# A two-block network on one core: a fixed TensorE order in the mixers' second stage, and earlier first outputs in the recurrent phase

## The chip, the cores and the metric

One core of one Trainium2 chip runs the whole program. The metric is the device time of one execution in microseconds (us). The kernel before takes 2088.3 us, the median of 3 runs (2087.17 to 2094.09). TensorE multiplies matrices, VectorE (DVE) and ScalarE (ACT) do the elementwise work, GpSimd (POOL) a little of it, and SyncE issues the loads of the weights.

## The reference

256 rows of 1024 features pass through ten phases in turn: attention, a feed-forward phase, a recurrent block, a feed-forward phase, and then twice a feed-forward phase, a hybrid mixer and a feed-forward phase. The change touches the recurrent block and the two mixers.

```python
def recurrent_block(h, w_in, conv_w, conv_b, w_a, b_a, w_x, b_x, lam, w_out):
    xr, gate = jnp.split(h @ w_in, 2, axis=-1)
    xr = centred_depthwise_conv(xr, conv_w, conv_b)
    y = rg_lru(xr, ..., reverse=False) + rg_lru(xr, ..., reverse=True)
    return (y * jax.nn.gelu(gate)) @ w_out

def hybrid_mixer(x, ...):
    ...
    ya = sliding_window_attention(...) @ w_branch_a
    ...
    o = gated_delta_rule(qb, kb, vb, g, beta)
    o = rms_norm(o) * dn_norm_g * jax.nn.silu(z)
    yb = o @ w_branch_b
    gate_a, gate_b = jnp.split(jax.nn.sigmoid(gate_raw), 2, axis=-1)
    return (gate_a * ya + gate_b * yb) @ w_out
```

The delta rule needs, for every head and chunk, the inverse of a lower triangular matrix; `t_inv` is applied to the values and the keys.

## The kernel before

All weights come as tiles of 128 x 1024 numbers in the order of use (`items_of`); `get` fetches them two at a time and splits each into a rounded half `hi` (ACT, L365) and a rest `lo` (DVE, L369), up to four tiles ahead of the one in use, into six buffers of each. A product of a weight tile is then three matmuls for every 128 rows, two with `hi` and one with `lo` (`up_mm`, L393 to L395; `mv_mm`, L429 to L431).

**Who sets the order.** The program is traced in the order of the Python code, and a list scheduler then places each engine's instructions by readiness and priority under its own cost model. Within a region under `tc.manual_schedule(engines={PE})` TensorE instead keeps the order of the code. An engine executes its own instructions strictly in the order placed.

**The mixers' second stage** (`ph_mix`, L1603 to L1618). `diag` inverts the 16 x 16 diagonal blocks of 16 units at once in 14 steps, each a shuffle (L1322), a multiply (L1323) and a subtract (L1324) on DVE. `blocks(0)` spreads the result into `B` (L1598). `double(bt)` then joins the blocks to 32, 64 and 128 in six steps: it transposes `B` into `D` on DVE (L1340), and alternates small matmuls of 32 x 32 or 64 x 64 (L1351, L1357 and L1360, L1370, L1381 and L1382, L1390, L1395, output `dq`) with copies and subtractions on DVE and ACT. `chunks(bt)` is the delta rule itself (L1415 to L1434, output `f`). `bt` is one of two halves of the heads. Between two of these steps stands `filler(1)`, one tile of work that depends on none of them: a branch product (output `py`, 24 matmuls), a quarter of z (output `z`, 12 matmuls of 512 columns), or a gate (output `pu`, 24 matmuls). Under the scheduler's free choice a filler may also run before the step that it follows in the code.

**The recurrent phase** (`ph_rnn`, L921 to L1078). For each of four groups of three channel tiles, `group` computes the two recurrences' gates by matmuls (output `gp`) and a long chain on ACT and DVE, `scans` runs six scans (L1029) and adds the two directions into `ys` (L1031), `gate(t)` makes one gate tile (`gl`, L1035), and `outs(g)` multiplies the two and splits the product into `tT` (ACT L382, DVE L384), which `down` multiplies into the four accumulators `acc` (L429 to L431, 12 matmuls for each of three tiles). In the code the order at the end is: `scans` of group 2, `group(3)`, `scans` of group 3, `outs(0)` and `down(0)`, three gates, `outs(1)` and `down(1)`, three gates, the rest.

Of the kernel before, what the change touches and what calls it, by code (L numbers as in the profile page):

```python
# [287 lines left out]
def fused_kernel(ctx, tc, x, wst, adaw, ada0, rows, rowc, cols, vecs, relb, cst, m1, rope, oh, out, phases=PH_ALL):  # L288
# [148 lines left out]
    def up(ph, *it):  # L437

        if (ph,) + it in head:
            return head.pop((ph,) + it)  # L440
        w = get(ph, *it)
        ps = ps_up()
        hT = state["hT"]
        if ph[:3] in ("mlp", "ffn"):
            up_wide(w, lambda kk: hT[:, kk, :], ps)
            return ps
        ps = ps[:, 0:256]
        if (ph,) + it in RAW:
            up_raw(w, ps)
        else:  # L450
            up_mm(w, lambda kk: hT[:, kk, :], ps)
        return ps
# [475 lines left out]
    def ph_rnn(ph, nxt):  # L928
# [91 lines left out]
        def scans():  # L1020

            g, rs, ii, aa = todo.pop()
            for d in range(2):
                r, i, a = rs[d], ii[d], aa[d]
                for t in range(3):
                    o, da, du = r[:, t, :], a[:, t, :], i[:, t, :]
                    if d == 1:
                        o, da, du = o[:, ::-1], da[:, ::-1], du[:, ::-1]
                    V.tensor_tensor_scan(out=o, data0=da, data1=du, initial=0.0, op0=ALU.mult, op1=ALU.add)  # L1029
            ys[g] = po.tile([128, 3, 256], F32, tag="ys", bufs=2, name="ys")  # L1030
            V.tensor_tensor(out=ys[g], in0=rs[0], in1=rs[1], op=ALU.add)  # L1031

        def gate(t):
            gl[t] = po.tile([128, 256], F32, tag="gl", bufs=6, name="gl")
            S.activation(out=gl[t], in_=up(ph, "g", t), func=AF.Gelu_apprx_tanh)  # L1035

        def outs(g):
            for tt in range(3):
                t = 3 * g + tt
                o = gl.pop(t)  # L1040
                V.tensor_tensor(out=o, in0=o, in1=ys[g][:, tt, :], op=ALU.mult)
                tT[t] = po.tile([128, 512], F32R, tag="tT", bufs=5, name="tT")
                split(tT[t][:, 0:256], tT[t][:, 256:512], o)
# [8 lines left out]
        while n < len(seq):  # L1052
            k, t = seq[n]
            if k == "x":
                conv(t)
            elif k == "b":
                if t:
                    scans()
                group(t // 3)
                if t == 9:  # L1060
                    scans()
                n += 2
            elif k == "g":
                gate(t)
                if t >= 10 and xs_todo:
                    xs_todo.pop(0)()
            else:
                g = t // 3
                outs(g)
                if g == 1:  # L1070
                    es.close()
                    xs_todo = x_scale()
                if g == 2:
                    for f in xs_todo:
                        f()
                    while side:
                        side.pop(0)()
                    ln_open(ph, nxt)  # L1078
                down(g)
                n += 2  # L1080
            n += 1
# [25 lines left out]
    def ph_mix(ph, nxt):  # L1107
# [291 lines left out]
        def chunks(bt):  # L1399

            H0 = 4 * bt
            A, ai, tl = fr[bt]
            C, v = BC[bt][1], vk[bt]
            m4 = lambda: p3.tile([128, 4, 128], F32, tag="m4", bufs=5, name="m4")

            def four(f):
                pv = ps_acc("f4").rearrange("p (u m) -> p u m", u=4)
                for h in range(4):
                    f(pv[:, h, :], h)
                return pv  # L1410
            w1, wt, kt = m4(), m4(), m4()
            for h in range(4):
                for c in range(2):
                    S.activation(out=v[:, h, c, :], in_=v[:, h, c, :], func=AF.Copy, scale=cf[:, c, H0 + h, 3:4])
            S.activation(out=kt, in_=four(lambda o, h: T.transpose(o, kq[H0 + h][:, 0, 0:128], idn)), func=AF.Copy)  # L1415
            S.activation(out=w1, in_=four(lambda o, h: T.matmul(o, lhsT=C[:, h, :], rhs=v[:, h, 0, :], start=True, stop=True)), func=AF.Copy)
            V.tensor_tensor(out=wt, in0=w1, in1=tl.unsqueeze(2).to_broadcast([128, 4, 128]), op=ALU.mult)
            yield
            S1 = m4()
            S.activation(out=S1, in_=four(lambda o, h: T.matmul(o, lhsT=kt[:, h, :], rhs=wt[:, h, :], start=True, stop=True)), func=AF.Copy)  # L1420
            V.tensor_copy(out=v[:, :, 0, :], in_=four(lambda o, h: T.matmul(o, lhsT=ai[:, h, :], rhs=w1[:, h, :], start=True, stop=True)))
            yield
            R, qs = m4(), m4()
            pk = four(lambda o, h: T.matmul(o, lhsT=kq[H0 + h][:, 0, 128:256], rhs=S1[:, h, :], start=True, stop=True))
            for h in range(4):
                V.scalar_tensor_tensor(out=R[:, h, :], in0=pk[:, h, :], scalar=cf[:, 1, H0 + h, 2:3], in1=v[:, h, 1, :], op0=ALU.mult, op1=ALU.add)
            pq = four(lambda o, h: T.matmul(o, lhsT=kq[H0 + h][:, 1, 128:256], rhs=S1[:, h, :], start=True, stop=True))
            V.tensor_tensor(out=qs, in0=pq, in1=eg[:, 1, H0:H0 + 4].unsqueeze(2).to_broadcast([128, 4, 128]), op=ALU.mult)
            yield
            w2 = m4()  # L1430
            S.activation(out=w2, in_=four(lambda o, h: T.matmul(o, lhsT=C[:, 4 + h, :], rhs=R[:, h, :], start=True, stop=True)), func=AF.Copy)
            yield
            po = four(lambda o, h: T.matmul(o, lhsT=ai[:, 4 + h, :], rhs=w2[:, h, :], start=True, stop=True))
            V.tensor_tensor(out=v[:, :, 1, :], in0=qs, in1=po, op=ALU.add)  # L1434
            yield

        def norm_o(cc):

            hs = slice(4 * cc, 4 * cc + 4)
            b4 = lambda m: m.unsqueeze(2).to_broadcast([128, 4, 128])  # L1440
            for c in range(2):
                o = vk[cc][:, :, c, :]
                sq = p3.tile([128, 4, 128], F32, tag="m4", bufs=5, name="sqo")
                f = p2.tile([128, 2, 4], F32, tag="f", bufs=2, name="f")
                q = qn[:, c, hs]
                S.activation(out=sq, in_=o, func=AF.Square)
                V.tensor_reduce(out=f[:, 0], in_=sq, axis=AX.X, op=ALU.add)
                V.tensor_tensor(out=f[:, 1], in0=q, in1=q, op=ALU.mult)
                V.scalar_tensor_tensor(out=f[:, 0], in0=f[:, 0], scalar=1.0 / 128.0, in1=f[:, 1], op0=ALU.mult, op1=ALU.mult)
                V.tensor_scalar(out=f[:, 0], in0=f[:, 0], scalar1=1e-6, scalar2=None, op0=ALU.add)  # L1450
                G.tensor_tensor(out=f[:, 0], in0=f[:, 0], in1=mhalf[:, 0:4], op=ALU.pow)
                V.scalar_tensor_tensor(out=f[:, 0], in0=f[:, 0], scalar=0.5, in1=q, op0=ALU.mult, op1=ALU.mult)
                V.tensor_tensor(out=o, in0=o, in1=b4(f[:, 0]), op=ALU.mult)
                V.tensor_tensor(out=o, in0=o, in1=zst[cc, c], op=ALU.mult)
# [23 lines left out]
        for j in range(3):  # L1478
            hi, lo = get(ph, "va", j)
            for kk in range(3 * j, min(3 * j + 3, 8)):  # L1480
                s = slice((kk - 3 * j) * VW, (kk - 3 * j) * VW + VW)
# [104 lines left out]
        def filler(n):  # L1586
            for _ in range(n):
                f = next(fi, None)
                if f:
                    f()  # L1590
# [5 lines left out]
        def blocks(bt):  # L1596
            B = p3.tile([128, 8, 32], F32, tag="B", name="B")
            V.tensor_tensor(out=B.rearrange("p u (e j) -> p u e j", j=16),  # L1598
                            in0=cs[:, K_P16:K_P16 + 32].rearrange("p (e j) -> p e j", j=16).unsqueeze(1).to_broadcast([128, 8, 2, 16]),
                            in1=dg["b"][:, 8 * bt:8 * bt + 8, :].unsqueeze(2).to_broadcast([128, 8, 2, 16]), op=ALU.mult)  # L1600
            BC[bt] = B, p3.tile([128, 8, 128], F32, tag="C", bufs=2, name="C")

        blocks(0)  # L1603
        filler(1)
        for _ in double(0):
            filler(1)
        blocks(1)
        steps = [double(1), chunks(0)]
        while steps:
            for s in list(steps):  # L1610
                if next(s, "end") == "end":
                    steps.remove(s)
            filler(1)
        norm_o(0)
        for _ in chunks(1):
            filler(1)
        filler(99)
        norm_o(1)  # L1618
        es3.close()
        es2.close()  # L1620
# [158 lines left out]
```

## Time and profile before

| | before |
|---|---|
| median of 3 runs | 2088.3 us |
| the profiled execution's own time | 2087.69 us |
| its span, first to last instruction | 2086.0 us |
| TensorE busy | 97% of the span |
| weight loads on TensorE | 85% |
| DVE, ACT, POOL busy | 73%, 54%, 6% |
| mean granted TensorE clock | 0.990 of full |

The span is what the trace covers; some 1.7 us lie around it. Busy time of TensorE is modelled, since matmuls overlap: 97% says that TensorE is rarely without work, not that it works at its peak. A stretch at a granted clock of 0.5 counts as busy and does half as much in it.

### The profile page before, as it was taken

What the parts mean: (1) busy time and instruction counts of PE and PEld (TensorE: products, weight loads), DVE (VectorE), ACT (ScalarE), POOL (GpSimd) and SP (SyncE); (2) the same over time, 40 slices, a digit from 0 to 9 for tenths busy, and PEclk for the clock granted to TensorE, in tenths of its full rate; (3) what the DMA queues carried; (4) which work ended last, traced back from release to release, by engine and by line L of the source; (5) the groups of instructions that cost most, each with busy time, mean ns of one, the idle gap of its engine ahead of it and who ended that gap; (6) DMA issues with size and microseconds to landing.
All of it is one profiled execution on the core that took longest, in us unless ns stands there. A gap on an engine that the chain in (4) does not pass through costs nothing. (4 is left out here: it accounts for less than half of the span.)

```text
span 2086.0 us, 34685 instructions
## 1 busy us (share of the span) xinstructions
PE 2027.6 (97%) x13786; PEld 1777.3 (85%) x13786; DVE 1516.6 (73%) x2735; ACT 1116.8 (54%) x1995; POOL 122.3 (6%) x157
## 2 busy tenths in 40 slices
PE   6999999989999999999999999999999999999998
PEld 4788888978888888888989888888889888998886
DVE  2689989987667666789956766676668897667665
ACT  3554446874544555477644455545546774445553
POOL 0000000000000000021011000000001111100000
PEclk9999999999999999999989999999999998999999
DMA  8978884355673655454424465555546434355552
GB/s 335 336 265 329 319 319 183 129 198 187 217 254 131 241 190 194 172 182 140 157 81 180 161 224 195 187 195 189 188 156 215 136 141 157 123 201 182 194 190 81
DMA packets 67698, 409.67 MB, mean 196 GB/s; under 512 B 8240, under 2 KB 8544, under 8 KB 27088
## 3 DMA queue, kind: packets, MB, share of 16 engines
q1 hardware_dynamic: 59952, 383.25, 50.5%
q0 software_dynamic: 7440, 24.03, 3.6%
q8 instruction: 108, 1.77, 0.3%
q14 instruction: 54, 0.44, 0.1%
q10 hardware_dynamic: 144, 0.18, 0.0%
HBM read 406.34 MB, written 4.24 MB: 197 GB/s over the span
## 5 line engine op out<-in xcount | busy, mean ns | idle before, releaser
L369 DVE TENSOR_TENSOR lo<-raw,hi 128x1024 fp32r<-128x1024 f32 (+2 forms) x689 | 729.1, 1069 | 308.8 <-ACT hi L365 299.1
L365 ACT ACTIVATE hi<-raw 128x1024 fp32r<-128x1024 f32 x578 | 605.3, 1053 | 338.2 <-PE pu L402 73.9
L402 PE MATMUL pu<-hT,hi 128*128 128x512 f32 x1760 | 439.2, 392 | 0.0
L402 PEld LDWEIGHTS pu<-hT,hi 128*128 128x128 f32 x1760 | 324.6, 188 | 65.2 <-issue 0.4
L429 PE MATMUL acc<-hi,tT 128*128 128x512 f32 x688 | 271.6, 396 | 3.2 <-ACT tT L382 3.0
L430 PE MATMUL acc<-hi,tT 128*128 128x512 f32 x688 | 271.6, 395 | 0.0
L393 PE MATMUL pu<-hT,hi 128*128 128x256 f32 x928 | 271.4, 292 | 0.0
L431 PE MATMUL acc<-lo,tT 128*128 128x512 f32 x688 | 270.2, 393 | 0.0
L395 PE MATMUL pu<-hT,lo 128*128 128x256 f32 x928 | 265.5, 286 | 2.3 <-DVE lo L369 2.3
L394 PE MATMUL pu<-hT,hi 128*128 128x256 f32 x928 | 265.5, 286 | 0.0
L404 PEld LDWEIGHTS pu<-hT,lo 128*128 128x128 f32 x1760 | 240.2, 191 | 17.1
L404 PE MATMUL pu<-hT,lo 128*128 128x256 f32 x1760 | 245.6, 283 | 0.0
L393 PEld LDWEIGHTS pu<-hT,hi 128*128 128x128 f32 x928 | 178.9, 193 | 12.9 <-issue 10.6
L382 ACT ACTIVATE tT<-r 128x256 fp32r<-128x256 f32 x152 | 63.1, 416 | 235.6 <-DVE r L918 136.9
L394 PEld LDWEIGHTS pu<-hT,hi 128*128 128x128 f32 x928 | 179.1, 193 | 3.0 <-issue 2.6
L395 PEld LDWEIGHTS pu<-hT,lo 128*128 128x128 f32 x928 | 178.9, 193 | 2.7 <-DVE lo L369 2.5
L429 PEld LDWEIGHTS acc<-hi,tT 128*128 128x128 f32 x688 | 130.0, 189 | 29.6 <-ACT tT L382 5.0
L431 PEld LDWEIGHTS acc<-lo,tT 128*128 128x128 f32 x688 | 129.8, 189 | 27.7 <-issue 0.4
L430 PEld LDWEIGHTS acc<-hi,tT 128*128 128x128 f32 x688 | 130.1, 189 | 24.4 <-DVE tT L384 1.6
L688 PE MATMUL hd<-h,raw 128*128 128x128 f32 x960 | 111.4, 276 | 0.0
L688 PEld LDWEIGHTS hd<-h,raw 128*128 128x128 f32 x960 | 109.5, 192 | 1.1
L384 DVE TENSOR_TENSOR tT<-r,tT 128x256 fp32r<-128x256 f32 x152 | 64.6, 426 | 54.8 <-ACT tT L382 54.8
(398 smaller groups left out, 2755.2 us busy)
## 6 DMA issues: line engine op xcount, KB each, us to landing
raw<-wst SPq DMA_DIRECT2D x316, 1024.0 KB, 4.8
aw<-adaw SPq DMA_DIRECT2D x80, 512.0 KB, 6.5
aw<-ada SPq DMA_DIRECT2D x16, 512.0 KB, 7.6
bias<-bias_d POOLq DMA_DIRECT2D x32, 192.0 KB, 2.8
g<-rows POOLq DMA_DIRECT2D x10, 512.0 KB, 4.7
b<-rows POOLq DMA_DIRECT2D x10, 512.0 KB, 5.7
bias_d<-ext_d POOLq DMA_DIRECT2D x1, 2048.0 KB, 20.2
gbc<-g_d POOLq DMA_DIRECT2D x4, 512.0 KB, 4.4
```

The costliest lines, as they stand in the source:

```text
L365: S.activation(out=hi[:, 0:n], in_=r, func=AF.Copy)
L369: V.tensor_tensor(out=lo[:, c:c + m], in0=r[:, c:c + m], in1=hi[:, c:c + m].bitcast(F32), op=ALU.subtract)
L384: (eng or V).tensor_tensor(out=dlo, in0=src, in1=dhi.bitcast(F32), op=ALU.subtract)
L393: T.matmul(ps, lhsT=hi[:, c], rhs=r[:, 0:256], start=kk == 0, stop=False)
L394: T.matmul(ps, lhsT=hi[:, c], rhs=r[:, 256:512], start=False, stop=False)
L395: T.matmul(ps, lhsT=lo[:, c], rhs=r[:, 0:256], start=False, stop=kk == KT - 1)
L402: T.matmul(ps, lhsT=hi[:, kk * 128:kk * 128 + 128], rhs=rhs(kk), start=kk == 0, stop=False)
L404: T.matmul(ps[:, 0:256], lhsT=lo[:, kk * 128:kk * 128 + 128], rhs=rhs(kk)[:, 0:256], start=False, stop=kk == KT - 1)
L429: T.matmul(ps, lhsT=th, rhs=hi, start=first, stop=False)
L430: T.matmul(ps, lhsT=tl, rhs=hi, start=False, stop=False)
L431: T.matmul(ps, lhsT=th, rhs=lo, start=False, stop=last)
L688: T.matmul(ps[:, half * 128:half * 128 + 128], lhsT=w[:, kk * 128:kk * 128 + 128], rhs=state["h32", half][:, kk, :], start=kk == 0, stop=k ...
```

## The change

Two independent edits. In both mixers the second stage goes under `tc.manual_schedule` for TensorE, so that `filler(1)` stays between the steps where the code has it. In the recurrent phase `outs(0)` moves ahead of `group(3)`, and `scans` of group 3 moves from right behind `group(3)` to behind the gate of tile 8. No arithmetic is added or removed.

```diff
             elif k == "b":
                 if t:
                     scans()
+                if t == 9:
+                    outs(0)
                 group(t // 3)
-                if t == 9:
-                    scans()
                 n += 2
             elif k == "g":
                 gate(t)
+                if t == 8:
+                    scans()
                 if t >= 10 and xs_todo:
                     xs_todo.pop(0)()
             else:
                 g = t // 3
-                outs(g)
+                if g:
+                    outs(g)
...
-        blocks(0)
-        filler(1)
-        for _ in double(0):
+
+        with tc.manual_schedule(engines={mybir.EngineType.PE}):
+            blocks(0)
             filler(1)
-        blocks(1)
-        steps = [double(1), chunks(0)]
-        while steps:
-            for s in list(steps):
-                if next(s, "end") == "end":
-                    steps.remove(s)
-            filler(1)
-        norm_o(0)
-        for _ in chunks(1):
-            filler(1)
-        filler(99)
+            for _ in double(0):
+                filler(1)
+            blocks(1)
+            steps = [double(1), chunks(0)]
+            while steps:
+                for s in list(steps):
+                    if next(s, "end") == "end":
+                        steps.remove(s)
+                filler(1)
+            norm_o(0)
+            for _ in chunks(1):
+                filler(1)
+            filler(99)
         norm_o(1)
```

Lines from L1062 on stand three, and from L1606 on five, higher in the changed kernel.

**First place: TensorE at the start of a mixer's second stage.** Before, from the first branch tile to the second step of `double(0)`; the lines left out are the rest of 96 matmuls `py` (four tiles), 48 `z` (four) and 11 `pu`:

```order
L393 MATMUL py<-oT,hi 128x256
...
L429 MATMUL z<-hi,hT 128x512
...
L393 MATMUL pu<-hT,hi 128x256
...
L1351 MATMUL dq<-D,A 32x16 x32
L395 MATMUL pu<-hT,lo 128x256
...
L1357 MATMUL dq<-P,B 32x16 x32
L1360 MATMUL dq<-B,P 32x16 x32
L1370 MATMUL dq<-D,A 32x32 x16
```

In the changed kernel, from the same branch tile; the lines left out are the rest of 48, 24 and 24 matmuls `py` (two tiles, one, one) and of 12 `z`:

```order
L393 MATMUL py<-oT,hi 128x256
...
L1354 MATMUL dq<-D,A 32x16 x32
L393 MATMUL py<-oT,hi 128x256
...
L1360 MATMUL dq<-P,B 32x16 x32
L1363 MATMUL dq<-B,P 32x16 x32
L393 MATMUL py<-oT,hi 128x256
...
L1373 MATMUL dq<-D,A 32x32 x16
L429 MATMUL z<-hi,hT 128x512
```

Ahead of the first step of `double(0)` stand two tiles where eight and a half stood, and behind every later step a whole tile. The other mixer reads the same.

**Second place: DVE at the end of `diag` in a mixer.** Before, from the eighth subtract to the transpose; left out are the steps between, with three more `lo`:

```order
L1324 TENSOR_TENSOR dgb<-dgb,dgs 128x16x8
L369 TENSOR_TENSOR lo<-raw,hi 128x1024
L1322 STREAM_SHUFFLE dgs<-dgb 128x256
...
L1323 TENSOR_TENSOR dgs<-dgs,dga 128x16x14
L369 TENSOR_TENSOR lo<-raw,hi 128x1024
L1324 TENSOR_TENSOR dgb<-dgb,dgs 128x16x14
L1598 TENSOR_TENSOR B<-cs,dgb 128x256
L1576 SCALAR_TENSOR_TENSOR zs<-zs,z 128x512
L1340 STREAM_TRANSPOSE D<-B 128x256
```

In the changed kernel; left out are only shuffles, multiplies and subtracts:

```order
L1327 TENSOR_TENSOR dgb<-dgb,dgs 128x16x8
L1325 STREAM_SHUFFLE dgs<-dgb 128x256
L1326 TENSOR_TENSOR dgs<-dgs,dga 128x16x9
...
L1327 TENSOR_TENSOR dgb<-dgb,dgs 128x16x14
L1601 TENSOR_TENSOR B<-cs,dgb 128x256
L1343 STREAM_TRANSPOSE D<-B 128x256
L1355 TENSOR_SCALAR P<-dq,cs 128x8x16
```

The five `lo` that stood between the last steps of `diag` now stand behind the transpose; up to the eighth multiply both orders are the same.

**Third place: DVE in the recurrent phase, behind the chain of the last group.** Before:

```order
L1014 SCALAR_TENSOR_TENSOR r<-q,r 128x768
L384 TENSOR_TENSOR tT<-gl,tT 128x256
L369 TENSOR_TENSOR lo<-raw,hi 128x1024
L1017 TENSOR_TENSOR i<-i,r 128x768 x2
L1029 SCALAR_TENSOR_TENSOR r<-a,i 128x256 x6
L369 TENSOR_TENSOR lo<-raw,hi 128x1024
L1031 TENSOR_TENSOR ys<-r 128x768
L369 TENSOR_TENSOR lo<-raw,hi 128x1024 x4
L384 TENSOR_TENSOR tT<-gl,tT 128x256 x3
```

In the changed kernel:

```order
L1014 SCALAR_TENSOR_TENSOR r<-q,r 128x768
L369 TENSOR_TENSOR lo<-raw,hi 128x1024 x2
L1017 TENSOR_TENSOR i<-i,r 128x768 x2
L369 TENSOR_TENSOR lo<-raw,hi 128x1024 x2
L1029 SCALAR_TENSOR_TENSOR r<-a,i 128x256 x2
L369 TENSOR_TENSOR lo<-raw,hi 128x1024 x2
L1029 SCALAR_TENSOR_TENSOR r<-a,i 128x256 x4
L384 TENSOR_TENSOR tT<-gl,tT 128x256
L1031 TENSOR_TENSOR ys<-r 128x768
L384 TENSOR_TENSOR tT<-gl,tT 128x256 x2
```

The third `tT` of the first outputs, the first `L384` before, has moved ahead of the whole chain of the last group, on ACT too; the six scans now let the `lo` of the gates through, and still stand ahead of the first `tT` of the second outputs.

## Rows read from the trace of the kernel before

**Rows 1.** The page, busy time of each engine:

```profile
PE 2027.6 (97%) x13786; PEld 1777.3 (85%) x13786; DVE 1516.6 (73%) x2735; ACT 1116.8 (54%) x1995; POOL 122.3 (6%) x157
```

**Rows 2.** Stretches of both mixers: us, busy PE PEld DVE ACT POOL, PEclk, DMA, GB/s:

```profile
1030.10:1048.60 18.50, 18.21 (x109) 16.12 (x108) 17.94 (x45) 8.41 (x9) 1.17 (x3) 1.00 0.65 227
1048.60:1069.50 20.90, 19.14 (x408) 17.32 (x408) 5.63 (x11) 7.42 (x15) 4.82 (x6) 0.59 0.26 96
1069.50:1119.50 50.00, 50.00 (x574) 47.13 (x575) 30.36 (x58) 23.56 (x37) 4.98 (x6) 1.00 0.31 111
...
1750.70:1769.30 18.60, 17.95 (x408) 16.28 (x408) 5.53 (x11) 7.31 (x15) 4.86 (x6) 0.63 0.28 107
```

**Rows 3.** The same view: stretches at one granted clock, and a wait without a fall:

```profile
126.00:140.00 14.00, 11.01 (x81) 9.76 (x80) 13.18 (x29) 8.69 (x14) 1.57 (x2) 1.00 0.32 112
...
434.66:438.07 3.41, 3.41 (x9) 2.69 (x9) 1.99 (x3) 3.38 (x4) 0.00 (x0) 0.50 0.16 29
444.90:448.31 3.41, 3.41 (x17) 3.41 (x17) 3.41 (x4) 1.56 (x3) 1.28 (x2) 0.50 0.22 23
1052.47:1069.54 17.07, 16.19 (x203) 14.61 (x204) 3.18 (x6) 6.35 (x13) 0.95 (x3) 0.50 0.19 63
1755.62:1769.27 13.65, 13.65 (x172) 12.35 (x171) 2.92 (x6) 5.25 (x10) 0.51 (x2) 0.50 0.22 78
```

**Rows 4.** Timeline of TensorE in both mixers: start, us, instruction, idle before it:

```profile
1024.34 0.36 PE L393 MATMUL py<-oT,hi 128*128 128x256 f32 x1
...
1030.17 0.28 PE L393 MATMUL py<-oT,hi 128*128 128x256 f32 x1
...
1119.50 0.27 PE L1462 MATMUL pt<-cs,vk 128*128 128x128 f32 x1
...
1726.45 0.36 PE L393 MATMUL py<-oT,hi 128*128 128x256 f32 x1
...
1819.33 0.27 PE L1462 MATMUL pt<-cs,vk 128*128 128x128 f32 x1
```

**Rows 5.** Timeline of DVE in the first mixer, the last steps of `diag`:

```profile
1032.38 1.21 DVE L369 TENSOR_TENSOR lo<-raw,hi 128x1024 fp32r<-128x1024 f32 x1
...
1034.04 0.29 DVE L1324 TENSOR_TENSOR dgb<-dgb,dgs 128x128 f32<-128x128 f32 x1
...
1039.00 0.45 DVE L1322 STREAM_SHUFFLE dgs<-dgb 128x256 f32<-128x256 f32 x1
1039.48 0.34 DVE L1323 TENSOR_TENSOR dgs<-dgs,dga 128x176 f32<-128x176 f32 x1
...
1041.75 0.36 DVE L1323 TENSOR_TENSOR dgs<-dgs,dga 128x192 f32<-128x192 f32 x1
1042.14 0.36 DVE L1324 TENSOR_TENSOR dgb<-dgb,dgs 128x192 f32<-128x192 f32 x1
...
1048.11 0.44 DVE L1340 STREAM_TRANSPOSE D<-B 128x256 f32<-128x256 f32 x1
```

**Rows 6.** Timeline of TensorE at the end of the recurrent phase:

```profile
434.46 1.93 PE L429 MATMUL acc<-hi,tT 128*128 128x512 f32 x4 [2.86 <-ACT tT L382]
...
444.70 0.43 PE L395 MATMUL pu<-hT,lo 128*128 128x256 f32 x1 [2.28 <-DVE lo L369]
...
451.56 0.63 PE L429 MATMUL acc<-hi,tT 128*128 128x512 f32 x2
...
459.96 0.28 PE L393 MATMUL pu<-hT,hi 128*128 128x256 f32 x1
```

**Rows 7.** Timeline of ACT and DVE there:

```profile
434.32 1.05 ACT L365 ACTIVATE hi<-raw 128x1024 fp32r<-128x1024 f32 x1
...
436.68 1.48 ACT L1015 ACTIVATE r<-r 128x1536 f32<-128x1536 f32 x1
...
439.94 3.59 DVE L1029 TENSOR_TENSOR_SCAN r<-a,i 128x256 f32<-128x256 f32 x6
...
449.97 1.09 DVE L384 TENSOR_TENSOR tT<-gl,tT 128x256 fp32r<-128x256 f32 x3
```

## The prediction, made before the changed kernel ran

> **What bounds the kernel now.** I read the page first: TensorE is busy 97% of the span [rows 1], so time can only be won where it waits or where its clock is low. I then asked for the busy time by stretch, for those whose granted clock is not 1.00. Besides the start and the end of the program there are four [rows 3]: two of 3.41 us in the recurrent phase and one in each mixer, of 17.07 and 13.65 us, all at 0.50, the lower of the clock's two levels (1.2 of 2.4 GHz). The reader is to see in rows 2 that the long ones lie right where `double(0)` runs: after 1048.6 TensorE is handed small matmuls with little between them, while in the 18.5 us ahead of that it is busy for 18.21 us with large tiles, and DVE is busy for 17.94. From 1069.5 to 1119.5 it is busy without a gap at the full clock. So the free order spends eight and a half fillers while `diag` is still being computed, and has few left for `double(0)`.
>
> The timeline gives each stage's length, from the first branch tile to the turn of the output: 1119.50 - 1024.34 = 95.16 us and 1819.33 - 1726.45 = 92.88 us [rows 4]. In the recurrent phase the timeline shows two waits [rows 6]: 2.86 us for the ACT half of the third `tT`, 2.28 us for the `lo` of a gate tile.
>
> **The mixers, step by step.** First what the stage costs without loss. In the first mixer 16.19 us of work are done at half the clock [rows 3], which at the full one take 8.1; 20.90 - 19.14 = 1.76 us are idle behind 1048.6 and 18.50 - 18.21 = 0.29 ahead of it [rows 2]. The loss is 8.1 + 1.8 + 0.3 = 10.2 us, and the work 95.2 - 10.2 = 85.0. The second mixer: 13.65 / 2 = 6.8, plus 18.60 - 17.95 = 0.65 and some 0.3, is 7.8; 92.9 - 7.8 = 85.1. Two counts that agree: 85 us of work, which the change leaves as it is.
>
> Next the new wait. TensorE now does two branch tiles, 1024.34 to 1030.17 [rows 4], and the next instruction needs `D`. When does `D` come? DVE's order is unchanged up to the eighth multiply, and none of its operations to there waits for more than those two tiles: the last `lo` is the one at 1032.38 [rows 5], whose buffer the second tile frees. From the eighth subtract at 1034.04 on, nothing but the chain is left in the new order. A step of it, each operation waiting for the one before, costs 0.48 (shuffle to multiply, 1039.00 to 1039.48), 0.39 (multiply to subtract, 1041.75 to 1042.14) and about as much from there to the next shuffle [rows 5]: 1.25 us. Six steps are 7.5, and with the eighth subtract (0.3), `B` and the transpose (0.45 each) `D` is there at 1034.04 + 0.3 + 7.5 + 0.9 = 1042.7; the reading goes by tenths, I take **1042.6**. That is six us earlier than the 1048.55 of before, since five `lo`, two `ya` and a `zs` no longer stand in the chain's way, but 12.4 us later than TensorE is free. Nothing else stands ahead in TensorE's order, so it idles for these 12.4 us; the fillers that covered them are queued behind the wait.
>
> Who waits with it: ACT is queued at the copies `C<-D`, which need the second step of `double(0)`, and the `hi` behind them wait too. This costs nothing at first: by then the buffers hold six tiles, `hi` and `lo`, for the six fillers of `double(0)`. A branch tile is 5.83 / 2 = 2.9 us [rows 4], the others much the same, and covers the copies between steps, as it does in `double(1)` before, which runs without a gap from 1069.5 on [rows 2]; so I cost the other steps' waits at nothing; were a filler not ready, one wait of about 1.1 us (a `lo` [rows 5]) would come back.
>
> Then the clock. A wait of 12.4 us is longer than any in the trace behind the start. Waits of 2.86 and 2.28 us [rows 6] were each followed by 3.41 us at 0.50 [rows 3]; the 2.99 idle us in the stretch from 126 to 140 were not. Behind the long wait come 64 small matmuls and a branch tile. The bounds for what the low clock costs there: nothing, as at 126; and 8.5 us, half of the 17.07. I take a low stretch of one and a half times 3.41 us, 5.2 us, hence **2.6 us** lost, being nearest to the rows where large tiles follow a wait.
>
> The Trainium skill speaks against the change here: TensorE: Matmul & The Clock Gate, section "HAM oscillation", holds that where TensorE waits between pieces of work its clock falls and each next piece starts at the low level. By that rule the 2.6 us are paid in both mixers, as I have it; by the row at 126 they would not be, and the sum would be 5.2 us less. The two rows in the recurrent phase agree with the rule, that one doesn't.
>
> A stage is then 85.0 + 12.4 + 2.6 = 100.0 us: **+4.8 us** on 95.2, and with 85.1, 100.1, **+7.2 us** on 92.9. The low stretches go, and a longer wait comes: what is late next is `D` itself.
>
> **The recurrent phase.** With `outs(0)` ahead of the last group, the third `tT` is ready long before its use, and the 2.86 us go; the twelve matmuls at 434.46 start at 431.6 and, at (459.96 - 451.56) / 36 = 0.233 us each [rows 6], end at 434.4. The first gate tile then meets its own weights: its `hi` is ACT's next, 434.3 to 435.4 [rows 7], its `lo` 1.1 us behind, 436.5. About 1.7 us of idle come back. Three gate tiles at 2.9 us run to some 445, their `lo` now let through between the scans. The second outputs need their first `tT`; DVE has it only behind `i` (after the square root, which ends at 438.2 before and some 0.9 us later now, one more `hi` standing ahead [rows 7]), six scans (3.6 us) and four more `lo`: 439.1 + 1.8 + 3.6 + 4 x 1.1, some 449. TensorE, which reached this place at 451.56 with `tT` ready from 449.97 on, now reaches it at 445 and waits about 3.5 us. From 449.4 the remaining 32 matmuls take 7.5 us, and 1.7 us more if this wait brings another 3.41 us of low clock: 458.5, against 459.96. Say **-1.8 us**; bounds: 0 when both waits lower the clock, -8.5 when neither wait nor low clock is left (2.86 + 2.28 + 3.41). Moved copies count nothing: ACT and DVE idle while TensorE works there.
>
> **Sum:** 4.8 + 7.2 - 1.8 = +10.2 us on the profiled execution's 2087.69, 2097.9; that execution lies 0.6 us under the median, and I put the forecast at **2098 us**. About 0.3%, 6.3 us, is what a measurement of this kernel can tell from no change.
>
> **Rivals.**
> - *Not slower: the recurrent phase gives back what the mixers lose.* Place: the second outputs. If their `tT` is ready when the third gate tile ends (445 instead of 449) and the first gate's `lo` when the first outputs end, all 8.5 us go: 12.0 - 8.5 = +3.5, 2091.2 us. For it: ACT and DVE have free time there. Against: six scans and four `lo` stand ahead of that `tT` in DVE's order. Chance 0.16.
> - *Faster: no wait for `D`.* The stages would cost 85 us each, -10.2 and -7.8, with the recurrent phase -19.8: 2068 us. It decides whether `D` comes by 1030.2. Against: DVE is busy for 17.94 of 18.50 us there [rows 2], and the steps of the chain wait for each other. The Trainium skill (TensorE: Matmul & The Clock Gate, section "A second HAM failure mode: psum-queue depth-cycling") blames a falling clock on many short idles between groups; by it dense tiles between the steps would end the low stretches, as this rival has it. Chance 0.06.
> - *Much slower: the low clock stays.* If `double(0)` keeps the clock at 0.50 as long as it does now, 8.5 us instead of 2.6 in each mixer: +11.8, 2110 us. For: the same small matmuls. Against: in `double(1)`, with tiles between its steps, the clock is 1.00 throughout [rows 2]. Chance 0.05.
>
> **How the numbers follow.** The forecast has 0.73. Its own range is 2092.7 (no low clock behind the waits) to 2104 (a low stretch of some 11 us in each mixer). The range of 8 in 10 takes in the first rival and half of the way to the last: 2090 to 2108. Faster by over 0.3% has 0.06; within 0.3%, that is under 2094.6, the first rival's 0.16 and 0.05 of the forecast's own low end, 0.21; slower 0.73.
>
> **What would show it.** In both mixers' timelines one idle stretch of 12 us in front of the first matmul of `double(0)`, its end following the transpose; `diag` ending six us earlier; full-clock work between the later steps; stages of 99 to 101 us. In the recurrent phase no wait for ACT at the first outputs and one of 3 to 4 us for DVE at the second. I am wrong if TensorE works within 3 us of the second branch tile, or if the stages come out under 95 us.

## The result, and the profile after

The changed kernel takes **2101.3 us**, the median of 5 runs (2094.9 to 2102.1); the kernel before, run beside it on the same chip, 2087.2 (2086.3 to 2094.1). The ratio is **1.0058, with an interval of 1.0042 to 1.0075**: slower, by 12 us of the 2087; the two medians lie some 14 us apart. The two profiled executions are 2101.58 and 2087.69 us, 13.9 apart. On the page TensorE is busy for five us less than in [rows 1], in a span 14 us longer:

```profile
PE 2022.7 (96%) x13786; PEld 1771.1 (84%) x13786; DVE 1521.0 (72%) x2735; ACT 1116.6 (53%) x1995; POOL 128.1 (6%) x157
```

TensorE's timeline (start, us, instruction, idle before it) of both mixers answers to [rows 4]:

```profile
1025.10 0.36 PE L393 MATMUL py<-oT,hi 128*128 128x256 f32 x1
...
1043.60 0.79 PE L1354 MATMUL dq<-D,A 32*32 32x16 f32 x45 [12.52 <-POOL B L1347]
...
1126.08 0.38 PE L1465 MATMUL pt<-cs,vk 128*128 128x128 f32 x2
...
1732.79 0.36 PE L393 MATMUL py<-oT,hi 128*128 128x256 f32 x1
...
1751.30 0.41 PE L1354 MATMUL dq<-D,A 32*32 32x16 f32 x15 [12.52 <-POOL B L1347]
...
1833.30 0.38 PE L1465 MATMUL pt<-cs,vk 128*128 128x128 f32 x2
```

A stage reads off as 1126.08 - 1025.10 = 100.98 us and 1833.30 - 1732.79 = 100.51 us, against 95.16 and 92.88. One idle stretch of 12.52 us stands in front of the first small matmul. The row names a POOL operation as what ended it; that one ends at 1043.09, and the transpose into `D`, the last row of DVE's timeline below, at 1043.29:

```profile
1034.57 0.29 DVE L1327 TENSOR_TENSOR dgb<-dgb,dgs 128x128 f32<-128x128 f32 x1
...
1034.90 0.43 DVE L1325 STREAM_SHUFFLE dgs<-dgb 128x256 f32<-128x256 f32 x1
1035.37 0.31 DVE L1326 TENSOR_TENSOR dgs<-dgs,dga 128x144 f32<-128x144 f32 x1
1035.72 0.31 DVE L1327 TENSOR_TENSOR dgb<-dgb,dgs 128x144 f32<-128x144 f32 x1
...
1041.95 0.39 DVE L1327 TENSOR_TENSOR dgb<-dgb,dgs 128x224 f32<-128x224 f32 x1
1042.38 0.42 DVE L1601 TENSOR_TENSOR B<-cs,dgb 128x256 f32<-128x256 f32 x1
1042.84 0.45 DVE L1343 STREAM_TRANSPOSE D<-B 128x256 f32<-128x256 f32 x1
```

The view by stretches (us, busy PE PEld DVE ACT POOL, PEclk, DMA, GB/s) answers to [rows 2, 3]:

```profile
1031.10:1043.60 12.50, 0.00 (x0) 0.03 (x1) 11.43 (x35) 1.06 (x1) 0.96 (x3) 0.58 0.38 144
1043.60:1050.10 6.50, 6.50 (x96) 6.24 (x100) 0.35 (x1) 0.21 (x1) 1.27 (x2) 0.50 0.01 3
1050.10:1126.10 76.00, 76.00 (x1001) 69.69 (x1002) 44.51 (x75) 37.69 (x60) 8.47 (x10) 1.00 0.36 129
...
22.66:26.07 3.41, 3.28 (x8) 2.53 (x8) 1.43 (x4) 2.54 (x7) 0.00 (x0) 0.50 1.03 420
36.31:43.14 6.83, 5.96 (x14) 4.79 (x15) 1.60 (x5) 3.15 (x8) 0.28 (x1) 0.50 0.47 172
...
135.30:138.71 3.41, 3.40 (x16) 3.40 (x17) 2.93 (x12) 1.96 (x5) 0.66 (x1) 0.50 0.00 0
452.74:456.15 3.41, 3.41 (x9) 2.64 (x10) 3.41 (x5) 0.98 (x2) 1.28 (x2) 0.50 0.23 79
1033.00:1050.07 17.07, 6.47 (x92) 6.24 (x96) 9.90 (x32) 0.18 (x1) 2.23 (x4) 0.50 0.18 64
1742.97:1756.63 13.66, 5.33 (x84) 5.33 (x85) 7.67 (x26) 0.00 (x0) 2.23 (x4) 0.50 0.14 56
```

While TensorE does nothing, DVE is busy for 11.43 of 12.50 us: up to the eighth subtract at 1034.57 with two `lo` and a `ya` among the steps of `diag`, from there on with the chain alone. The low clock begins inside the wait and outlasts it: of its 17.07 us, 6.47 us are work, which at the full clock would take half, so 3.2 us are lost; in the second mixer 5.33 / 2 = 2.7. From 1050.1 to the turn TensorE is busy for 76.00 of 76.00 us at the full clock.

In the recurrent phase, TensorE's timeline against [rows 6]:

```profile
438.60 0.39 PE L393 MATMUL pu<-hT,hi 128*128 128x256 f32 x1 [0.69 <-ACT hi L365]
...
439.55 0.39 PE L393 MATMUL pu<-hT,hi 128*128 128x256 f32 x1 [0.45 <-ACT hi L365]
...
450.29 0.39 PE L393 MATMUL pu<-hT,hi 128*128 128x256 f32 x1 [0.69 <-ACT hi L365]
...
452.57 0.67 PE L430 MATMUL acc<-hi,tT 128*128 128x512 f32 x1 [1.77 <-DVE tT L384]
...
461.68 0.28 PE L395 MATMUL pu<-hT,lo 128*128 128x256 f32 x1
...
487.08 0.66 PE L661 MATMUL pt<-cs,X 128*128 128x128 f32 x4 [0.28 <-ACT X L652]
```

The last group's gates began at 416.76 before and at 420.05 now. From there to the tile behind the second outputs it is 459.96 - 416.76 = 43.2 us before and 41.6 now; to the first transposes of the norm behind the phase (at 486.58 before) 69.8 and 67.0.

The 13.9 us between the profiled executions are, in order of time:

| stretch | us |
|---|---|
| start to the last group's gates | +3.3 |
| from there to the first mixer's second stage (recurrent edit: -2.8) | -2.5 |
| second stage, first mixer | +5.8 |
| from its end to the second mixer's second stage | -0.2 |
| second stage, second mixer | +7.6 |
| the rest | -0.1 |

The +3.3 us lie in instructions that the change leaves alone, where three stretches at half clock (at 22.66, 36.31 and 135.30) stand that the profile of before hasn't.

### The profile page after: what moved, and what is told of

The parts are those of the page before. It is cut to its first block, busy times and chain, and to the rows that moved or that the text cites. A ratio compares the mean times of both kernels' runs of the same rounds, so it can differ in the third digit from the quotient of the medians.

```text
span 2099.9 us, 34686 instructions
## 1 busy us (share of the span) xinstructions
PE 2022.7 (96%) x13786; PEld 1771.1 (84%) x13786; DVE 1521.0 (72%) x2735; ACT 1116.6 (53%) x1995; POOL 128.1 (6%) x157
## 5 line engine op out<-in xcount | busy, mean ns | idle before, releaser
L384 DVE TENSOR_TENSOR tT<-r,tT 128x256 fp32r<-128x256 f32 x152 | 64.5, 425 | 53.7 <-ACT tT L382 53.7
```

The costliest lines, as they stand in the source:

```text
L384: (eng or V).tensor_tensor(out=dlo, in0=src, in1=dhi.bitcast(F32), op=ALU.subtract)
```

## The experiments

Stages are told as in the table: from the first branch tile to the turn of the output. "Work" is a stage less its idle time and half of the busy time at the low clock; it is 84.9 to 85.9 us in every kernel here (in the one with useless matmuls without their 11.1 us).

**Each edit alone.** First the fixed order in the mixers, the last part of the diff above; then its first three parts, the recurrent edit.

> The kernel before with the fixed order in both mixers alone; the recurrent phase as before. Theory (the mixers carry all of the loss, 5.8 us in the first and 7.6 in the second by the two traces; the prediction had 4.8 and 7.2): 13.4 us slower than before, some 2100.6 us, with an idle stretch of 12.5 us ahead of the first matmul of double(0) in both mixers. Rival 1 (the recurrent edit is part of the loss): 10 us slower or less, 2097 or less. Rival 2 (the 3.3 us that the changed kernel's profile lost ahead of the recurrent phase come from the change): they show here again, in code that is the same, and the run is 16 to 17 us slower. If they are chance, they don't come regularly.

Measured: 2101.5 us, ratio 1.0075 (1.0052 to 1.0098). Stages of 100.18 and 102.35 us with waits of 12.52 and 13.80 us. In the second one DVE stood still for 1.17 us ahead of the eighth multiply: a `lo` stands there, its `hi` was late, and ACT had waited for that `hi`'s weights. TensorE's wait is longer by 1.3:

```profile
1750.98 0.20 PE L1351 MATMUL dq<-D,A 32*32 32x16 f32 x1 [13.80 <-POOL B L1344]
```

So what stands ahead of `D` on DVE comes out on TensorE. The last group's gates began at 417.65, 0.9 us later than before and not 3.3, with code that is the same up to there; two of the three early stretches at half clock stand here too. The mixers carry the loss.

> The kernel before with the recurrent edit alone; mixers under the scheduler's free choice. Theory: the phase gains 1.6 us from the first gate matmul of the last group to the next gate tile (43.2 us before, 41.6 in the changed kernel), so 2085.6 us against 2087.2; the waits at the first gate tile (1.1 us), the second outputs (2.5 us) and one low clock stretch of 3.41 us behind it stay. Rival 1 (the phase can give back all of 2.86 + 2.28 + 3.41 us): 2078.7. Rival 2 (the new waits bring two low clock stretches again): 2087 or a little more, no gain.

Measured: 2085.8 us, ratio 0.9992 (0.9976 to 1.0007): no difference that a measurement shows, but in the profile the norm's first transposes come 68.2 us behind the start of the last gates, against 69.8. The waits are 0.70, 0.45, 0.71 and 1.75 us, with 6.83 us at half clock around and behind the last. The theory holds by the rows; that all 8.5 us are to be had does not.

**One of the recurrent edit's two moves, and one move more.** First `scans` of the last group goes back to where it stood:

```diff
                 group(t // 3)
+                if t == 9:
+                    scans()
                 n += 2
             elif k == "g":
                 gate(t)
-                if t == 8:
-                    scans()
```

> The first of the recurrent edit's two moves alone: the first outputs ahead of the last group, the scans where they stood before, right behind it. Theory (the two waits of the kernel before have two causes, one for each move): the wait of 2.86 us at the first outputs goes, TensorE comes to the gate tiles earlier by as much, and the lo that stand behind the six scans are late by some 4 to 5 us instead of 2.28: no gain, 2086.5 to 2087.5. Rival (the outputs' place is all of the gain): 2085.7 as with both moves.

Measured: 2087.9 us, ratio 1.0003 (0.9992 to 1.0013). The wait at the first outputs is gone, and the gate tile waits for its `lo` behind the scans:

```profile
446.51 0.39 PE L395 MATMUL pu<-hT,lo 128*128 128x256 f32 x1 [3.20 <-DVE lo L369]
...
487.27 0.33 PE L661 MATMUL pt<-cs,X 128*128 128x128 f32 x1 [2.78 <-ACT X L652]
```

3.20 us instead of 2.28 [rows 6], where 4 to 5 were expected, and the norm waits 2.78 us instead of 1.27: one move alone only shifts the wait. Then `scans` goes the other way, behind `outs(1)`:

```diff
                 gate(t)
-                if t == 8:
-                    scans()
...
                 if g == 1:
+                    scans()
                     es.close()
```

> The kernel with the recurrent edit alone, and the scans of the last group moved once more, behind the second outputs. Theory (the wait of 1.75 us at the second outputs is DVE's six scans standing ahead of their tT, and it lowers the clock for 3.41 to 6.83 us): wait and low stretch go, 1.8 + 1.7 to 3.4 us below 2085.8, so 2081 to 2082.5. Rival (the scans only change place: the third or fourth outputs, or the norm behind the phase, wait instead): no gain, 2085 to 2087.

Measured: 2083.1 us, ratio 0.9981 (0.9970 to 0.9992): faster, and 0.6 us short of the theory's range. The wait at the second outputs is 0.65 us, no stretch of the phase is at half clock, and the norm comes after 65.8 us. A wait of 1.19 us stands at the third outputs instead.

**More tiles ahead of `D`.** In the fixed order:

```diff
             blocks(0)
-            filler(1)
+            filler(5)
...
-            steps = [double(1), chunks(0)]
+            steps, turn = [double(1), chunks(0)], True
...
-                filler(1)
+                turn = not turn
+                filler(1 if turn else 0)
```

> The changed kernel with six tiles instead of two ahead of the first matmul of double(0), in the same fixed order; the four tiles are taken from between the steps of double(1) and chunks(0), where only every second step is followed by one. Theory: a tile ahead takes 2.92 us of TensorE but puts its lo (1.07 us on DVE) and a share of the ya into the chain's way, so that each shortens the wait for D by some 1.7 us only: 12.5 - 4 x 1.7 = 5.7 us idle in each mixer, the low clock behind it as now, and the tiles taken away are not missed, since double(1) and chunks(0) cover each other: 2101.3 - 2 x 6.8, some 2088 us. Rival 1 (DVE runs the chain first, D is not later): the wait shrinks to under 1 us and the low clock goes: 2101.3 - 2 x 14.5, some 2072 us. Rival 2 (the steps without a tile wait themselves): four waits of 1 to 2 us in each mixer come back, 2095 to 2102 us.

Measured: 2095.5 us, ratio 1.0043 (1.0027 to 1.0059). Stages of 98.72 and 99.55 us. The waits in the first, from TensorE's timeline:

```profile
1044.71 0.25 PE L1354 MATMUL dq<-D,A 32*32 32x16 f32 x4 [5.59 <-POOL B L1347]
...
1074.50 0.38 PE L1423 MATMUL f<-m,m 128*128 128x128 f32 x1 [0.95 <-DVE m L1420]
...
1090.38 0.27 PE L1393 MATMUL dq<-C,A 64*64 64x64 f32 x1 [1.43 <-DVE C L1386]
```

5.59 us for `D`, and 6.19 in the second mixer, where 5.7 was expected: a tile ahead is 2.8 us of TensorE's work and makes `D` 1.1 to 1.2 us later. But 2.4 us of waits come back where tiles were taken away and 0.52 at a step of `double(0)`, and the low clock, now behind two waits, costs 4.6 and 5.0 us instead of 3.2 and 2.7. The two stages together gain 3.2 us and not 13.6; the rest of the 5.8 in the median is not theirs. Fillers moved about are paid for elsewhere: the theory is right on the wait for `D`, the second rival on the steps without a tile.

**Is it the wait that lowers the clock?** TensorE gets work of no use while it waits:

```diff
-            for _ in double(0):
+            for n, _ in enumerate(double(0)):
                 filler(1)
+                if n == 0:
+                    pw_ = ps_up("wk")
+                    for k in range(48):
+                        T.matmul(pw_, lhsT=hT[:, k % 8, 0:128], rhs=hT[:, k % 8, :], start=True, stop=True)
```

> The changed kernel with 48 more matmuls of 512 columns in each mixer between the second branch tile and the first matmul of double(0); their result is not used. TensorE is busy where it idled, with 48 x 0.233 = 11.2 us of work that the output does not need. Theory (the wait lowers the clock, and the clock then costs 3.2 and 2.7 us): D comes at the same time, the stretches at half clock (17.07 and 13.65 us in the changed kernel) go, and the kernel gets 5.9 us faster with more work: some 2095.4 us. Rival 1 (the small matmuls of double(0) lower the clock, whatever stood ahead of them): the low stretch begins behind them instead, no gain, 2101. Rival 2 (the clock is not what is slow there, the steps wait for each other): full clock, and no gain either, 2101.

Measured: 2095.4 us, ratio 1.0044 (1.0029 to 1.0059). The number is the theory's, but its reason gives about a third of it: the stages are 99.71 and 99.68 us, together 2.1 us shorter and not 5.9, and the rest of what the profile gains lies ahead of the mixers (the last gates begin at 415.34). The 48 matmuls took 11.1 us, 1.55 us of idle were left, and behind those came a low stretch:

```profile
1025.20:1036.30 11.10, 11.09 (x50) 8.85 (x48) 10.34 (x33) 1.06 (x1) 0.00 (x0) 1.00 0.49 174
1036.30:1037.85 1.55, 0.00 (x1) 0.04 (x2) 1.26 (x3) 0.00 (x0) 0.86 (x3) 1.00 0.00 0
1038.87:1042.28 3.41, 3.41 (x19) 3.41 (x18) 0.10 (x1) 0.00 (x0) 0.35 (x1) 0.50 0.02 5
```

So the low clock shrinks with the wait, from 3.2 and 2.7 us of loss to 1.7 in each mixer. A low stretch still follows the short wait, and it begins right behind the small matmuls, as the first rival has it; this run alone doesn't tell the two apart, the halves below do. The 11.1 us of useless work in each mixer cost no time: `D` came as late as without them.

**`D` in time.** `diag` inverts each half of the units by itself, with tiles of its own (the second half's in a pool that stays open through the second stage), the first half as soon as its `A` is there:

```diff
-        def diag():
-            ac, bc, sh = dg["a"], dg["b"], dg["s"]
+        def diag(bt):
+            ac, bc, sh = (dg[k + str(bt)] for k in "abs")
...
-                if b == 1:
-                    todo.extend([lambda: next(dg["steps"], 0)] * 5)
+                todo.extend([lambda n=n: [next(dgs[b], 0) for _ in range(n)] for n in ((2, 2, 1) if b == 0 else (1,) * 5)])
```

> The kernel with the recurrent edit and free mixers, but diag inverts the two halves of the units apart: the first half in the first stage, right after its A is there, the second half where all of it ran before. D of the first half no longer has to wait for the last steps. Theory (D's late coming is what both orders suffer from: the free order spends its fillers on it and has none for the steps, the fixed order waits): D is there when TensorE comes, the scheduler itself places a whole tile between the steps, and both mixers fall to the 85.2 us of work: 9.1 + 7.9 us (94.29 and 93.05 us now) below the 2085.8 of the recurrent edit, less what 42 more small DVE operations in each first stage (some 0.25 us each, half of them not hidden at worst) cost: 2069 to 2079, say 2070. Rival 1 (without a fixed order the steps still run with little between them at the low clock): stages of 90 us and more, 2080 or above. Rival 2 (the first stage waits for DVE): 10 us longer in each mixer, 2085 or above.

> The changed kernel (fixed order in both mixers) with diag in halves as in the run before. Theory: the idle stretch of 12.5 us in front of the first matmul of double(0) and the low clock behind it go in both mixers, stages of 85.2 us: 15.8 + 15.3 us below the 2101.3 of the changed kernel, 2070; the same as with the free order, since the two orders come out alike once D is there. Rival 1 (the fixed order is worth something by itself): 5 us or more below the free order with halves. Rival 2 (another operand of the first steps is late too, so that the wait stays in part): 2075 to 2090, with an idle stretch of 3 to 9 us in the same place.

Measured: 2080.7 us, ratio 0.9972 (0.9961 to 0.9983), with the free order; 2081.5, ratio 0.9969 (0.9957 to 0.9981), with the fixed one. Stages of 88.87 and 85.71 us, and of 87.34 and 85.70. The transpose into `D` starts at 1027.46, and in the kernel with the fixed order the first small matmul follows its tile without a wait. The stage as a whole (columns as in the view by stretches) has the clock at 1.00:

```profile
1031.81 0.20 PE L1352 MATMUL dq<-D,A 32*32 32x16 f32 x2
...
1025.88:1113.22 87.34, 85.85 (x1139) 79.16 (x1139) 56.25 (x119) 42.09 (x67) 10.68 (x14) 1.00 0.37 136
```

The 1.49 us that are idle in this stage lie within one step; the second mixer has none. The free order has 1.63 us at the same step, the second row, and 3.41 us at half clock from 1041.22 on:

```profile
1038.01 0.44 PE L1361 MATMUL dq<-B,P 32*32 32x16 f32 x32 [1.49 <-issue]
```

```profile
1041.33 0.62 PE L1361 MATMUL dq<-B,P 32*32 32x16 f32 x32 [1.63 <-issue]
```

The profile names nothing that these wait for. But with the fixed order its record of transfers has 16 KB on the queue for instructions from 1035.69 to 1036.65, and the idle stretch ends 1.36 us behind that. Nine of the kernels here, the one before among them (1.71 us, to 1053.35), have one such stretch in the first mixer, of 1.16 to 1.88 us, and each ends 1.30 to 1.57 us behind such a transfer: it looks as if TensorE waits for its instructions there, though no run tests it.

The clock is 1.00 through the same small matmuls in both mixers of the fixed order: without a wait ahead of them and with tiles between, they don't lower it, and the first rival of the run with useless matmuls is out. Whether bare ones do by themselves no run tests. With the free order the scheduler itself now places a tile between the steps. The late `D` is thus what both orders paid for, one with low clock between bare steps, the other with a wait; the fixing adds nothing of its own. Of the 10 us missing to the expected 2070 most stand in the first stages: from the first mixer's turn to the second's branch tiles it is 611.1 and 610.9 us against 606.9 before, the way from the last group's gates to the first mixer grew by 4.2 and 3.7 us against the same kernels without halves, and the first mixer's second stage is 2 to 4 us longer than the 85.2 of the sum. The first stages have new waits for DVE's `vt`:

```profile
979.04 0.33 PE L1176 MATMUL pt<-cs,vt 128*128 128x128 f32 x1 [1.63 <-DVE vt L1170]
...
998.95 0.33 PE L1176 MATMUL pt<-cs,vt 128*128 128x128 f32 x1 [1.44 <-DVE vt L1170]
```

That was the second rival of the run with the free order, at some 4 us instead of 10 in each mixer.

**Taking work off DVE, twice without success.** First the multiplies and subtracts of the first half on POOL, with the scans behind `outs(1)`:

```diff
+            E = V if bt else G
...
-                V.tensor_tensor(out=sh[:, :, 0:j], ...
-                V.tensor_tensor(out=bc[:, :, 0:j], ...
+                E.tensor_tensor(out=sh[:, :, 0:j], ...
+                E.tensor_tensor(out=bc[:, :, 0:j], ...
```

> The kernel with halves and free mixers, with two edits more: the first half's multiplies and subtracts run on POOL, which is busy for 6% (29 of the 43 operations leave DVE in each first stage), and the scans of the last group stand behind the second outputs. Theory (what the halves lost was DVE's time in the first stage, where it is busy for 103.7 of 114.3 us in the kernel before and 106.7 with halves, and which grew by 4.2 to 4.3 us in each mixer): the 8.5 us come back, and 2.7 us for the scans (2085.8 to 2083.1): 2080.7 - 11.2, some 2069.5 us. Rival 1 (each shuffle on DVE waits for POOL, and what is queued behind it waits too, the more so as POOL takes longer for one such operation): the first stages stay as long or get longer, 2078 or above. Rival 2 (POOL's work slows DVE's beside it): a part only, 2073 to 2078.

Measured: 2088.6 us, ratio 1.0018 (1.0005 to 1.0032). The stages are 87.13 and 85.72 us, but the stretch between them grows to 614.2. The first rival: in the first mixer DVE's shuffles wait 3.9 us in all for POOL's subtracts, and TensorE 2.39 us in one place for an `sq` that ACT makes of DVE's `kq`, with a low stretch behind it. How much of it is the second rival's, this run doesn't separate.

Then, all of `diag` on DVE again and the scans behind `outs(1)`, without and with this edit:

```diff
-                    V.tensor_tensor(out=lo[:, c:c + m], ...
+                    (G if st[j][1] == "qa" and st[j][2] >= 3 else V).tensor_tensor(out=lo[:, c:c + m], ...
```

> Halves on DVE, free mixers, and the scans of the last group behind the second outputs: the two edits that each were faster. Theory (they lie in different phases and add up): 2080.7 - 2.7 = 2078.0 us. Rival (the gain of the scans was chance; in the run with POOL the third outputs waited 1.69 us and a low stretch came behind that): 2080 to 2082.

> As the run with halves and later scans, and the lo of five tiles of each mixer (qa 3 to 7, spread over the first stage) are subtracted on POOL instead of DVE. Unlike the steps of diag these don't go back and forth: DVE waits for none of them, and TensorE needs each only three tiles later. Theory: 5 x 1.07 us of DVE are free in each first stage, against the 4.3 us that the halves cost it: 2078.0 - 8.5, some 2070 us. Rival 1 (POOL takes so long for 1024 columns that TensorE waits for the lo; zs of 512 columns takes 1.7 us on POOL, so 3.4 us are to be expected, and 8 tiles of TensorE's work stand between two of them): 2078 or above. Rival 2 (DVE's other operations get slower beside POOL): 2074 to 2078.

Measured: 2079.7 us, ratio 0.9972 (0.9962 to 0.9983), without, and 2093.6, ratio 1.0038 (1.0024 to 1.0052), with POOL. In the first, the scans' gain did not add up: the third outputs waited 1.72 us and 3.41 us at half clock followed, as the rival has it; its 2079.7 lie between the two forecasts. In the second the stretch between the stages is 617.9 us, against 610.8 in the first. A `lo` takes 2.39 us on POOL, less than the 3.4 expected; POOL's timeline and then DVE's show what it did:

```profile
943.05 2.37 POOL L369 TENSOR_TENSOR lo<-raw,hi 128x1024 fp32r<-128x1024 f32 x1
```

```profile
942.79 2.67 DVE L1212 SCALAR_TENSOR_TENSOR cf<-nrmk,cf 128x8 f32<-128x8 f32 x1
945.38 0.16 DVE L1214 TENSOR_SCALAR cf<-cf 128x8 f32<-128x8 f32 x1
945.45 0.22 DVE L1236 TENSOR_SCALAR sm<-sm,vc 128x2 f32<-128x2 f32 x1
945.59 0.16 DVE L1213 SCALAR_TENSOR_TENSOR cf<-eg,cf 128x8 f32<-128x8 f32 x1
```

An operation on eight columns, 0.16 us a little later, takes 2.67 us and ends with POOL's. Beside each of POOL's ten `lo` one operation of DVE is held so, until 0.01 to 0.14 us behind the `lo`; the five so held in a mixer take 9.8 us together, for the 5 x 1.07 that were to be saved. It is the second rival's mechanism at more than its size, since 2093.6 is far above the 2078 that it allowed; the first rival's wait for the `lo` itself is not there. The three versions with halves on DVE are the fastest here, some 6 us below the kernel before; which is best of them these runs don't tell, and the interval of the later scans alone (0.9970 to 0.9992) overlaps theirs.

## Why the prediction was right

The measured ratio makes 12.1 us (8.8 to 15.7); the prediction had 10.2, and 2101.3 us lies in its range. The mechanism is the forecast one, a wait for `D` in both mixers; that the sum came so close is in part luck, since the mixers were forecast too low and the recurrent phase's gain too low as well. Its steps:

- **Work of a stage, 85.0 us:** 85.2 and 85.3 in the changed kernel, and within 1 us of it wherever the order went.
- **When `D` comes:** from the eighth subtract to the end of the transpose 8.7 us were forecast, and 1043.29 - 1034.57 = 8.72 came; a chain step is (1041.95 - 1034.57) / 6 = 1.23 us for 1.25. The wait of 12.4 us came as 12.52 in both mixers. That the waiting is for the chain the halves show.
- **No wait at the other steps:** right; behind the first wait TensorE is busy without a gap in both stages. It needs a tile at every step, as the run with four of them taken away shows.
- **The low clock, 2.6 us:** 3.2 and 2.7. This is the term that was sized too low. The prediction took a low stretch of 5.2 us behind the wait; 6.5 and 5.3 came, as the tail of one that began inside the wait.
- **Mixers +12.0 in sum:** +13.4; of the 1.4 too few, 0.7 are the low clock, 0.2 the waits, and 0.5 the work of the stages.
- **Recurrent phase, -1.8 us:** -1.6 at the place that it named; its own figures, 458.5 against 459.96, make -1.5. The split was other than forecast. The first gate tile waited 1.14 us for 1.7, TensorE around the second outputs 2.46 (0.69 of it for the next gate's `hi`) for 3.5, and one low stretch of 3.41 came as forecast. It left out the norm behind the phase, whose wait fell from 1.27 to 0.28 us, so that the edit is worth 2.8. With the mixers that makes +10.6: the mixers' 1.4 too few and the phase's 1.0 too few cancel for the most part.
- **The rest of the 13.9,** 3.3 us, was not forecast and is not the change: the run with the useless matmuls has all of the change and came to the same place at 415.34, earlier than the kernel before.

Of the rivals, the low clock did not stay: 3.2 and 2.7 us are lost and not 8.5; the recurrent phase gave back a third of what the first rival needed; and the case of no wait for `D` is what the halves made of it, whose stages, 87.3 and 85.7 us with the fixed order, bear its price of 85 nearly out; in the changed kernel its condition was not met. The Trainium skill's rule (TensorE: Matmul & The Clock Gate, section "HAM oscillation"), that pieces of work behind a wait start at the low clock, agrees with both mixers, where 6.47 and 5.33 us of work behind 12.52 us of idle ran at 0.50. What its section "A second HAM failure mode: psum-queue depth-cycling" holds of frequent short idles between groups is not settled here: with tiles between the steps and no idle the clock was 1.00 from 1050.1 to the turn, but in the second mixer of the kernel before it stood at 0.50 for 13.65 us in which TensorE was busy throughout [rows 3]. What held it down there stays open.

## What to carry to other kernels

A scheduler that spends its fillers early may be covering for an operand that comes late; hold the fillers back and the same lateness stands there as a wait. Ask first when that operand can be there and what on its engine stands ahead of it, and move the order only then. A filler hides its own length less what it puts on the engine that the late chain runs on (here 2.8 us less 1.1 to 1.2).

## What the runs showed of the hardware

- Beside a `lo` on POOL, an operation of DVE with two inputs in SBUF was held until POOL's was done: 2.67 us for eight columns. The same at another place: with POOL's `lo` from 968.27 to 970.66, DVE's operation on two columns ended at 970.68 after 1.40 us. The Trainium skill (SBUF — State Buffer, section "Who interferes with whom") has the two engines lock each other out for a whole instruction; the trace agrees, ten times out of ten. Reductions of DVE with one input ran on beside such a `lo`, in 0.29 and 0.41 us at 922.42 and 922.62.
- The same wait is followed by a low clock in one execution and not in the next: the 2.94 us in front of the norm at 130 left it at 1.00 in the profile of before and were followed by 3.41 us at 0.50 in that of the changed kernel. Idle stretches of 1.49 and 1.70 us at one step of `double(0)` left it up, with 1.63 us at the same step it fell, and with 1.16 us in the run with `lo` on POOL 3.41 us at 0.50 came 1.0 us later. What decides is not settled here; executions of one kernel differ by several us, and a gain of 2 us is read from rows better than from medians.
